# A recurrence's spilled tiles: later loads in longer pieces, values at the sixth phase, scales for two units at a time

## The chip, the cores and the metric

The kernel runs on one core of one Trainium2 chip. The metric is the device time of one execution in microseconds (us). TensorE (PE) multiplies matrices, VectorE (DVE), ScalarE (ACT) and GpSimd (POOL) work element by element, and SyncE (SP) issues nearly all DMAs. "PEld" in the profile is TensorE's loading of the stationary operand, which overlaps its matmuls.

## The reference

The model has two layers over 256 tokens of width 2048: an RWKV-7 mixer with a recurrent state per head, and a sparse attention mixer. Only the first layer's recurrence and what feeds it matter here. It is, per head of size 64:

```
def wkv7_scan(r, w, k, v, a, b):
    def step(S, inp):
        r_t, w_t, k_t, v_t, a_t, b_t = inp
        sa = einsum('bhvk,bhk->bhv', S, a_t)
        S = S * w_t[:, :, None, :] + sa[..., None] * b_t[:, :, None, :] + v_t[..., None] * k_t[:, :, None, :]
        return S, einsum('bhvk,bhk->bhv', S, r_t)
    ...
o = (o - mean) * rsqrt(var + GN_EPS) * ln_g + ln_b
o = (o + sum(r * k * r_k) * v) * silu(z)
y = o @ w_o
```

There are 32 heads. The projections r, k, v, z are products of the mixed input with four 2048x2048 matrices, and `w_o` is another.

## The kernel before, in words

The kernel computes in chunks of 64 tokens, four chunks in all, so the recurrence turns into small matmuls. Two column blocks of 128 (four heads) make a **unit**; there are eight units, U = 0 to 7, and x = 0 or 1 names a block in a unit. An earlier stage has already made, for every block, a tile with four parts (transformed keys, cumulated decays, a scaled key and the removal vectors) and has **spilled** it to DRAM as `spd`, 128 rows of 1284 values each. The values v and the gate z lie in DRAM as `vd` and `zd`.

The recurrence's loop runs over units, and in each over 12 **phases** v = 0 to 11: three for each chunk. In a phase the program writes, one after the other, the phase's own small matmuls with their copies (`phase`), the preparation of the next unit (`prep`), the normalization of the unit before (`finish`), loads, and then `fill(n)`, which puts in n steps of dense matmuls: first the projection r (`pair_block`, lines L1249 to L1251), then the output product. In this part the instructions of all five engines stay in the order in which the program writes them. SP is an engine like the others here: a DMA whose turn has not come, because the one ahead of it waits, is not issued.

What the change touches and what reads it:

- `load_spl` (L998, L1002) brings the spilled tile of unit U into `SPL[U % 2]`. Unit 0 and unit 1 come before the loop, each as two whole tiles of 642 KB. In the loop unit U + 2 comes during unit U, one piece of a fifth of a tile in each of the phases 0 to 9. The first 512 of the 1284 columns are read by `prep` steps "B0" and "B1" (phases 2 and 4 of the unit before), the rest by `scale_r` (L1035 to L1038, phase 6 of the unit before) and by steps "A0" and "A1" behind it (L1080, L1082, phases 7 and 9).
- `load_v` (L1007) brings the values of unit U + 1 into `UV` in phase 0 of unit U; the matmuls L1097 read them from phase 0 of unit U + 1.
- `load_gb` brings `a_ln_g` and `a_ln_b`, repeated over 64 partitions, into `gb` (runs of 64 values, 256 bytes). In unit 0, phases 8 to 11, it loads those of units 0 to 5; those of units 6 and 7 come in phase 10 of units 2 to 5. Steps "b" (L1181) and "g" (L1183) of the unit after read them.
- `load_rows` (L1019, L1021) brings v and z again for the normalization, in phases 8 and 9. Its first DMA waits for the unit before to be done with the tile.
- The weights come as pieces `wraw` of 512 KB (L179) into five buffers; ACT makes the high part `whi` of each (L207) and DVE the low part `wlo` (L192), three half-pieces ahead of the matmuls. A new piece can be issued when DVE has read the old one in its buffer.

While the first units run, DVE also works off a triangular inversion in the background (L849 to L885).

Of the kernel before, what the change touches and what calls it, by code (L numbers as in the profile page):

```python
# [218 lines left out]
def hybrid_kernel(ctx: ExitStack, tc: tile.TileContext, a: dict, out: bass.AP):  # L219
    nc = tc.nc  # L220
# [48 lines left out]
    def store_heads(d, nb, tt, t, eng):  # L269
        for i in range(2):  # L270
            dst = bass.AP(tensor=d.tensor, offset=d.offset + 4 * nb * 128 * T + (2 * tt + i) * CH,
                          ap=[[T, 64], [64 * T, 8], [1, 64]])
            eng.dma_start(dst, t[64 * i:64 * i + 64, :].rearrange("p (n d) -> p n d", d=64))
# [52 lines left out]
    for ph in QZ:  # L326
        if ph < 10:
            c0 = 128 * QB0[ph]
# [212 lines left out]
    def prep(kp):  # L541
        if kp == 2:
            banks(tp=(6,))
        px = turned_x[kp] if kp < 2 else turn_x(kp)
        for i in range(2) if kp else ():
            k = 2 * kp + i
            sl = px[:, i * 256:i * 256 + 256]
            norm_x(k, sl, G)
# [150 lines left out]
    SPW = 512 + NCH * (CH + 1) + 256 + 256  # L699
# [206 lines left out]
    H = lambda x, h: R[h ^ x]  # L906
    NU = NK // 2
# [6 lines left out]
    def load_a(U, which="AT"):  # L914
        sch.require(lambda: "T" not in which or U // 4 in tdone)
        for x in range(2):
            for h in range(2):
                j, at = 2 * U + x, 64 * (h ^ x) + 32
                if "A" in which:
                    d = abdd[j // 8][1]  # L920
                    src = bass.AP(tensor=d.tensor, offset=d.offset + (j % 8 * 8 + h) * 2048, ap=[[32, 32], [4096, NCH], [1, 32]])
                    G.dma_start(A10[at:at + 32, x, :, 0:32], src)
                if "T" in which:
                    G.dma_start(T00[64 * h:64 * h + 32, x, :, 0:32], inverse(tnd[U // 4], (j % 8) * 2 + h, 0))

    def load_y(U, eng=G, qs=(1, 0)):
        sch.require(lambda: U // 4 in tdone)
        for q in qs:
            for x in range(2):
                for h in range(2):  # L930
                    at = 64 * (h ^ x) + 32 * q
                    eng.dma_start(Yb[U % 2][at:at + 32, x, :, 32 * q:32 * q + 32],
                                inverse(yvd[U // 4], ((2 * U + x) % 8) * 2 + h, q))
# [54 lines left out]
    each = [(x, h) for x in range(2) for h in range(2)]  # L988
# [1 line left out]
    in_order = ExitStack()  # L990
    in_order.enter_context(tc.manual_schedule(engines={e.engine for e in (PE, V, S, G, nc.sync)}))

    SPLIT = (0, 256, 512, 772, 1028, SPW)

    def load_spl(U, pieces=range(10)):
        if len(pieces) == 10:
            for x in range(2):
                nc.sync.dma_start(SPL[U % 2][x][:, :SPW], spd[2 * U + x])  # L998
            return
        for i in pieces:  # L1000
            x, c0, c1 = i // 5, SPLIT[i % 5], SPLIT[i % 5 + 1]
            nc.sync.dma_start(SPL[U % 2][x][:, c0:c1], spd[2 * U + x][:, c0:c1])  # L1002

    def load_v(U, eng=nc.sync):
        for x in range(2):
            for h in range(2):
                eng.dma_start(UV[U % 2][R[h], 1 - x, h], vd[2 * U + x, R[h], :].rearrange("p (c d) -> p c d", c=NCH))  # L1007

    gb = one("gb", [128, 2, 12, 64])

    def load_gb(U, nu, part):
        for x, h in part:
            for i, v in enumerate((a["a_ln_g"][0], a["a_ln_b"][0])):
                src = bass.AP(tensor=v.tensor, offset=v.offset + U * 256 + x * 128 + h * 64, ap=[[0, 64], [256, nu], [1, 64]])
                nc.sync.dma_start(gb[H(x, h), i, x:2 * nu:2], src)

    def load_rows(t, d, U):
        flat = t.rearrange("p x c d -> p x (c d)")
        nc.sync.dma_start(flat[:, 0], d[2 * U])  # L1019
        for h in range(2):  # L1020
            nc.sync.dma_start(flat[H(1, h), 1], d[2 * U + 1, R[h]])  # L1021
# [8 lines left out]
    def scale_r(U, x):  # L1030
        if x == 0:
            PCH[U] = scan.tile([128, 2, NCH], F32, name="pc", bufs=3)
        BK, pp, kr, ar = parts(U, x)
        pr = rps[U % 2][:, 256 * x:256 * x + 256]
        V.tensor_tensor(ar[:, 1], c3(pr), pp[:, :, 1:], op=OP.mult)  # L1035
        V.tensor_tensor(mb[:, x], pr, kr, op=OP.mult)
        G.tensor_copy(PCH[U][:, x], pp[:, :, CH])
        G.tensor_tensor(ARS[U % 2][x], ar[:, :, 1:, :],  # L1038
                        pp[:, None, 0:NCH - 1, CH:CH + 1].to_broadcast([128, 2, NCH - 1, CH]), op=OP.mult)
# [103 lines left out]
    def stats(U, c):  # L1143
        if c == 0:
            STA[U] = (scan.tile([128, 2, 4, 6], F32, name="sta", bufs=2), scan.tile([128, 2, 4, 2], F32, name="mv", bufs=2))
        src = view(U, 192 + 64 * c, 64) if U == NU - 1 else OU[U][:, :, 64 * c:64 * c + 64]
        for x in range(2):
            V.bn_stats(STA[U][0][:, x, c, :], src[:, x])
# [44 lines left out]
    def turn_y(U):  # L1193
        yt = [PBK[U][:, x * 512:x * 512 + 256] for x in range(2)]
        for i in range(NCH):
            for x, h in each:
                r = H(x, h)
                PE.matmul(yt[x][R[h], i * 64:i * 64 + 64], OU[U][r, x, 64 * i:64 * i + 64], ident[r, r], start=True, **mm)
        made = [ring("y", 2 * U + x) for x in range(2)]
        for x, (yh, yl) in enumerate(made):  # L1200
            S.activation(yh, yt[x], AF.Copy)
            mixed[("y", 2 * U + x)] = (yh, yl)
        for x, (yh, yl) in enumerate(made):
            V.tensor_tensor(yl, yt[x], yh.bitcast(F32), op=OP.subtract)
        sch.t += 350
# [59 lines left out]
    def fill(n):  # L1265
        budget[0] += 3 * N256 * n
        while budget[0] > 1.0:
            c = next(dense)
            budget[0] -= c
            sch.t += c  # L1270
            sch.pump()

    W.late = True
    load_spl(0)
    load_y(0, G, (1,))
    load_a(0, "A")
# [8 lines left out]
    G.memset(Yb[1], 0.0)  # L1285
    load_y(1)
    fill(8)
    load_spl(1)
    fill(8)
    PBK[1] = pair_tile(1)  # L1290
    for step in PROLOGUE:
# [15 lines left out]
    for U in range(NU):  # L1307
        PBK[U] = pair_tile(U % 2)
        P = U - 1
        PACE[0] = PACES[min(U + 1, 3)]  # L1310
        for v in range(12):
            HOLD[0] = U > 0 and v in (0, 1, 2, 11)
            phase(U, v // 3, v % 3)
            if v % 3 == 2 and U == NU - 1:
                stats(U, v // 3)
            sch.pump()
            if v == 10 and U + 2 < NU:
                load_y(U + 2, qs=(1,))
            if v == 11:
                finish(U, "copy")  # L1320
                if U == NU - 1:
                    finish(U, "rg")
            if v == 0:
                if U and U + 1 < NU:
                    load_y(U + 1, qs=(0,))
                if U + 1 < NU:
                    load_v(U + 1)
            if U == 0 and v == 2:
                PACE[0] = 0.0
                for _ in range(9):  # L1330
                    sch.pump()
                PACE[0] = PACES[1]
            if v < 10 and U + 2 < NU:
                load_spl(U + 2, (v,))
            if v == 6 and U + 1 < NU:
                scale_r(U + 1, 0)
                scale_r(U + 1, 1)
            for step in AUX.get(v, ()):
                if step == "T":
                    if U:  # L1340
                        turn_y(P)
                elif U + 1 < NU:
                    prep(step, U + 1)
            if U:
                for step in NORM.get(v, ()):
                    finish(P, step)
            if v == 3 and U == 0:
                for tt in range(2):
                    store_heads(zd, 3, tt, z3[tt], G)
            if v > 7 and U == 0:  # L1350
                load_gb(0, 6, each[v - 8:v - 7])
            if v == 10 and U in (2, 3, 4, 5):
                load_gb(6, 2, each[U - 2:U - 1])
            if v == 5 and U + 2 < NU:
                load_a(U + 2, "AT" if U != 2 else "A")
            if v == 8 and U == 2:
                load_a(U + 2, "T")
            if v == 8:
                load_rows(vt, vd, U)
            if v == 9:  # L1360
                load_rows(zt, zd, U)
            fill(FILLO if U + 1 == NU else FILLL[v] if U + 2 == NU else FILL[v])
            sch.pump()
    U = NU - 1
# [541 lines left out]
```

## Time and profile before

| what | value |
|---|---|
| median of 3 runs | 1115.77 us (1111.92 to 1116.19) |
| profiled execution | 1113.02 us, its span 1111.2 us |
| granted TensorE clock | 0.998 |
| busy share of the span: PE, PEld, DVE, ACT, POOL | 98%, 86%, 76%, 65%, 31% |
| `spl` pieces in the loop | 60 DMAs of 128 or 130 KB |
| whole `spl` tiles ahead of the loop | 4 DMAs of 642 KB |

The recurrence lies between about 340 and 560 us of the span. A view "by windows" gives the busy time of each engine in each stretch; "waits" says what ended an engine's idle time; the "timeline" lists instructions by start, with the idle time ahead of them in brackets. "Landing" of a DMA is the time from its issue to its data being there. A matmul's modelled end lies some 0.16 us after the next one's start, so that short holes between matmuls do not show as idle time.

### The profile page before, as it was taken

How to read it: one execution, taken by the hardware profiler on the slowest of the kernel's cores; microseconds unless marked ns; L12 is line 12 of the kernel's file. 1: busy time of each engine (PE TensorE's matmuls, PEld its weight loads, DVE VectorE, ACT ScalarE, POOL GpSimd, SP SyncE). 2: the span in 40 equal slices, each digit the busy share in tenths (PEclk: the TensorE clock that was granted, in tenths of full speed). 3: DMA queues.
4: the chain of work that ended last, by engine and by line, in shares of the span. 5: the costliest groups of instructions: out<-in, count | busy, mean ns of one | idle time of the engine just before them, and what ended most of it. 6: DMA issues, size and time to landing. Idle time of an engine off the chain costs nothing.

```text
span 1111.2 us, 25246 instructions
## 1 busy us (share of the span) xinstructions
PE 1088.1 (98%) x9232; PEld 954.0 (86%) x9232; DVE 840.4 (76%) x1784; ACT 724.7 (65%) x1737; POOL 344.3 (31%) x423
## 2 busy tenths in 40 slices
PE   8999999999999899999999999999999999999997
PEld 7788899888889888999888888888989999988886
DVE  6999976679887897666667876765677988886564
ACT  7767777666775457656557766665657677775453
POOL 1300036424348557763200110101323334342012
PEclk9999999999999999999999999999999999999999
DMA  7458888877879968765578667675745354745753
GB/s 260 153 193 246 237 213 252 243 191 218 254 228 266 255 181 242 230 180 150 169 240 276 199 201 258 196 262 164 202 142 150 103 150 127 187 109 197 276 184 107
DMA packets 221837, 224.74 MB, mean 202 GB/s; under 512 B 48240, under 2 KB 173264, under 8 KB 221328
## 3 DMA queue, kind: packets, MB, share of 16 engines
q1 hardware_dynamic: 216384, 217.60, 65.9%
q0 software_dynamic: 4864, 4.92, 1.7%
q8 instruction: 73, 1.20, 0.5%
q10 hardware_dynamic: 464, 0.59, 0.2%
q14 instruction: 52, 0.43, 0.1%
HBM read 200.49 MB, written 22.58 MB: 201 GB/s over the span
## 4 chain that ended last, share of the span: by engine, by line
PE 57%; DVE 3%; ACT 1%; issue 1%; DMA 0%; POOLq 0%; POOL 0%; DVEq 0%; ACTq 0%
PE bank L617 8%; PE bank L616 8%; PE bank L619 8%; PE bank L1647 5%; PE bank L235 5%; PE bank L1648 3%; DVE wlo L192 2%; PE bank L1249 2%; PE bank L1250 1%; PE bank L1251 1%; PE pair L619 1%; PE pair L616 1%; PE pair L617 1%; PE bank L1215 1%; ACT whi L207 1%
## 5 line engine op out<-in xcount | busy, mean ns | idle before, releaser
L192 DVE TENSOR_TENSOR wlo<-wraw,whi 128x512 fp32r<-128x512 f32 (+2 forms) x616 | 443.8, 734 | 145.4 <-ACT whi L207 141.4
L207 ACT ACTIVATE whi<-wraw 128x512 fp32r<-128x512 f32 (+2 forms) x664 | 401.7, 618 | 180.8 <-PE bank L619 66.4
L192 POOL TENSOR_TENSOR wlo<-wraw,whi 128x512 fp32r<-128x512 f32 (+2 forms) x48 | 61.9, 1290 | 172.6 <-ACT whi L207 131.3
L617 PE MATMUL bank<-wlo,mh 128*128 128x512 f32 (+1 forms) x288 | 109.5, 382 | 1.3 <-DVE wlo L192 1.2
L617 PE MATMUL bank<-wlo,mhl 128*128 128x512 f32 (+2 forms) x288 | 108.0, 375 | 0.0
L619 PE MATMUL bank<-whi,ml 128*128 128x512 f32 (+1 forms) x288 | 107.9, 379 | 0.0
L619 PE MATMUL bank<-whi,mhl 128*128 128x512 f32 (+2 forms) x288 | 107.3, 373 | 0.0
L616 PE MATMUL bank<-whi,mhl 128*128 128x512 f32 (+2 forms) x288 | 99.5, 373 | 0.3 <-ACT Vt L1529 0.3
L616 PE MATMUL bank<-whi,mh 128*128 128x512 f32 (+1 forms) x288 | 91.9, 380 | 0.3 <-ACT whi L207 0.2
L1647 PE MATMUL bank<-mhl,whi 128*128 128x512 f32 x256 | 91.9, 397 | 0.0
L1249 PE MATMUL bank<-mhl,whi 128*128 128x256 f32 x256 | 77.9, 304 | 1.4 <-issue 1.4
L617 PE MATMUL bank<-wlo,kvh 128*128 128x512 f32 x192 | 76.0, 396 | 0.0
L619 PE MATMUL bank<-whi,kvl 128*128 128x512 f32 x192 | 75.3, 392 | 0.0
L634 PE MATMUL bank<-mh,whi 128*128 128x256 f32 x256 | 74.8, 292 | 0.4 <-ACT whi L207 0.4
L636 PE MATMUL bank<-mh,wlo 128*128 128x256 f32 x256 | 73.1, 288 | 0.6 <-DVE wlo L192 0.6
L635 PE MATMUL bank<-ml,whi 128*128 128x256 f32 x256 | 72.9, 285 | 0.0
L1648 PE MATMUL bank<-mhl,wlo 128*128 128x256 f32 x256 | 72.9, 285 | 0.0
L1251 PE MATMUL bank<-mhl,wlo 128*128 128x256 f32 x256 | 72.2, 282 | 0.2 <-DVE wlo L192 0.2
L1250 PE MATMUL bank<-mhl,whi 128*128 128x256 f32 x256 | 72.1, 282 | 0.0
L616 PE MATMUL bank<-whi,kvh 128*128 128x512 f32 x192 | 66.7, 391 | 0.0
L617 PEld LDWEIGHTS bank<-wlo,mh 128*128 128x128 f32 x288 | 54.1, 188 | 12.1 <-DVE wlo L192 2.5
L619 PEld LDWEIGHTS bank<-whi,ml 128*128 128x128 f32 x288 | 54.2, 188 | 9.5
(383 smaller groups left out, 2743.9 us busy)
## 6 DMA issues: line engine op xcount, KB each, us to landing
wraw<-in_a_w_rkvz_dram SPq DMA_DIRECT2D x128, 512.0 KB, 5.2
wraw<-in_kv_w_dram SPq DMA_DIRECT2D x48, 512.0 KB, 4.5
wraw<-in_b_w_in_dram SPq DMA_DIRECT2D x40, 512.0 KB, 4.3
wraw<-in_a_w_o_dram SPq DMA_DIRECT2D x32, 512.0 KB, 4.7
wraw<-in_b_w_o_dram SPq DMA_DIRECT2D x32, 512.0 KB, 4.2
spd<-sp SPq DMA_DIRECT2D x16, 642.0 KB, 4.9
wraw<-in_b_w_in_dram SPq DMA_DIRECT2D x24, 384.0 KB, 3.2
wraw<-in_cmp_w_dram SPq DMA_DIRECT2D x16, 512.0 KB, 3.9
```

Source lines behind the costliest of these rows:

```text
L192: eng.tensor_tensor(lv, src, hv.bitcast(F32), op=OP.subtract)
L207: self.nc.scalar.activation(hv, src, AF.Copy)
L616: PE.matmul(o, mh[:, ts], wh[:, 0, :], start=k == ends[0], stop=False)
L617: PE.matmul(o, mh[:, ts], wl[:, 0, :], start=False, stop=False)
L619: PE.matmul(o, ml[:, ts], wh[:, 0, :], start=False, stop=k == ends[1])
L634: PE.matmul(o, wh[:, s, :], mh, start=k == 0 and first, stop=False, **kw)
L636: PE.matmul(o, wl[:, s, :], mh, start=False, stop=k == NK - 1, **kw)
L1249: PE.matmul(oo, wh[:, i, c], mh, start=k == 0 and x == 0, stop=False, **kw)
L1250: PE.matmul(oo, wh[:, i, c], ml, start=False, stop=False, **kw)
L1251: PE.matmul(oo, wl[:, i, c], mh, start=False, stop=k == NK - 1, **kw)
L1647: PE.matmul(o, wh[:, s, :], beside[("u", k)], start=k == 0, stop=False)
L1648: PE.matmul(o[:, :T], wl[:, s, :], mh, start=False, stop=k == NK - 1)
```

## The change

The split of a tile is coarser: three pieces of 512, 516 and 256 columns in place of five. The pieces 0 and 3 (the first 512 columns of both blocks) of unit U + 2 are loaded in phases 6 and 8 of unit U. The other four are loaded in phases 0 to 3 of unit U + 1, the unit whose `scale_r` in phase 6 reads them. Unit 1 gets its pieces 0 and 3 ahead of the loop and the other four in unit 0, where it was loaded whole ahead of the loop. The values are loaded in phase 5 rather than 0. Units 0, 1 and 2 load `gb` for two units each in phases 8 to 11, where unit 0 loaded six.

```
-    SPLIT = (0, 256, 512, 772, 1028, SPW)
+    SPLIT = (0, 512, 1028, SPW)
...
-            x, c0, c1 = i // 5, SPLIT[i % 5], SPLIT[i % 5 + 1]
+            x, c0, c1 = i // 3, SPLIT[i % 3], SPLIT[i % 3 + 1]
...
-                nc.sync.dma_start(gb[H(x, h), i, x:2 * nu:2], src)
+                u0 = U % 6
+                nc.sync.dma_start(gb[H(x, h), i, 2 * u0 + x:2 * (u0 + nu):2], src)
...
-    load_spl(1)
+    load_spl(1, (0, 3))
...
-                if U + 1 < NU:
-                    load_v(U + 1)
...
-            if v < 10 and U + 2 < NU:
-                load_spl(U + 2, (v,))
+            if v < 4 and U + 1 < NU:
+                load_spl(U + 1, ((1, 2, 4, 5)[v],))
+            if v in (6, 8) and U + 2 < NU:
+                load_spl(U + 2, (3 * (v - 6) // 2,))
...
-            if v > 7 and U == 0:
-                load_gb(0, 6, each[v - 8:v - 7])
+            if v > 7 and U < 3:
+                load_gb(2 * U, 2, each[v - 8:v - 7])
...
+            if v == 5 and U + 1 < NU:
+                load_v(U + 1)
```

The order of instructions on PE, DVE, ACT and POOL is the same before and after; only SP's changes. SP, from the last loads ahead of the loop through unit 0 (`spl_4694` and `spl_4695` are the two blocks of odd units, `spl_4557` and `spl_4558` those of even ones), before:

```order
L998 DMA spl_4694<-spd 128x1284
L998 DMA spl_4695<-spd 128x1284
L179 DMA wraw<-in_a_w_rkvz_dram 128x4x256 x3
L1007 DMA uv_4698<-vd 64x256 x4
L1002 DMA spl_4557<-spd 128x256 x2
L179 DMA wraw<-in_a_w_rkvz_dram 128x4x256
L1002 DMA spl_4557<-spd 128x260
L1002 DMA spl_4557<-spd 128x256 x2
L1002 DMA spl_4558<-spd 128x256
L179 DMA wraw<-in_a_w_rkvz_dram 128x4x256
```

and now:

```order
L1002 DMA spl_4694<-spd 128x512
L1002 DMA spl_4695<-spd 128x512
L179 DMA wraw<-in_a_w_rkvz_dram 128x4x256 x3
L1002 DMA spl_4694<-spd 128x516
L1002 DMA spl_4694<-spd 128x256
L179 DMA wraw<-in_a_w_rkvz_dram 128x4x256
L1002 DMA spl_4695<-spd 128x516
L1002 DMA spl_4695<-spd 128x256
L1007 DMA uv_4698<-vd 64x256 x4
L179 DMA wraw<-in_a_w_rkvz_dram 128x4x256
```

Of unit 1's two tiles, two fifths stay ahead of the loop, and the rest takes the place where unit 2's pieces stood; the values follow behind them. SP in unit 4, from its last weight piece of the unit before to the weight piece of phase 5, before:

```order
L179 DMA wraw<-in_a_w_rkvz_dram 128x4x256
L1007 DMA uv_4698<-vd 64x256 x4
L1002 DMA spl_4557<-spd 128x256 x2
L179 DMA wraw<-in_a_w_rkvz_dram 128x4x256
L1002 DMA spl_4557<-spd 128x260
L1002 DMA spl_4557<-spd 128x256 x2
L1002 DMA spl_4558<-spd 128x256
L179 DMA wraw<-in_a_w_rkvz_dram 128x4x256
```

and now:

```order
L179 DMA wraw<-in_a_w_rkvz_dram 128x4x256
L1002 DMA spl_4694<-spd 128x516
L1002 DMA spl_4694<-spd 128x256
L179 DMA wraw<-in_a_w_rkvz_dram 128x4x256
L1002 DMA spl_4695<-spd 128x516
L1002 DMA spl_4695<-spd 128x256
L1007 DMA uv_4698<-vd 64x256 x4
L179 DMA wraw<-in_a_w_rkvz_dram 128x4x256
```

The pieces between the weight pieces are now those of unit 5, which the same unit's phase 6 reads, and no longer those of unit 6; the four loads of values have moved from ahead of them to behind them.

More of the change, by code (lines that the diff above doesn't have):

```diff
@@ L991, in hybrid_kernel, with load_spl @@
     in_order.enter_context(tc.manual_schedule(engines={e.engine for e in (PE, V, S, G, nc.sync)}))
-    SPLIT = (0, 256, 512, 772, 1028, SPW)
-    def load_spl(U, pieces=range(10)):
-        if len(pieces) == 10:
+    SPLIT = (0, 512, 1028, SPW)
+    def load_spl(U, pieces=None):
+        if pieces is None:
             for x in range(2):
```

## The prediction

> **What bounds the kernel now.** I read the page's first lines, then the busy time by windows over the recurrence, then TensorE's waits in it.
>
> ```profile
> span 1111.2 us, 25246 instructions
> PE 1088.1 (98%) x9232; PEld 954.0 (86%) x9232; DVE 840.4 (76%) x1784; ACT 724.7 (65%) x1737; POOL 344.3 (31%) x423
> ```
>
> TensorE is idle for 23.1 of 1111.2 us. The change moves DMAs of the recurrence alone, so what it can win lies there. Columns after the length: busy us of PE, PEld, DVE, ACT, POOL, then clock, DMA share, GB/s.
>
> ```profile
> 340.00:360.00 20.00, 20.00 (x273) 19.32 (x273) 13.63 (x29) 11.57 (x24) 16.00 (x32) 1.00 1.05 272
> 360.00:380.00 20.00, 18.52 (x397) 16.80 (x390) 16.64 (x57) 8.63 (x24) 10.48 (x19) 1.00 1.04 294
> 380.00:400.00 20.00, 18.61 (x377) 16.79 (x377) 16.89 (x49) 11.11 (x32) 12.94 (x18) 1.00 0.87 211
> 400.00:420.00 20.00, 17.84 (x390) 15.91 (x388) 19.50 (x46) 9.30 (x27) 9.83 (x16) 1.00 0.53 156
> 420.00:440.00 20.00, 19.98 (x425) 18.16 (x426) 16.92 (x40) 14.55 (x39) 13.85 (x25) 1.00 0.85 249
> 500.00:520.00 20.00, 20.00 (x381) 18.19 (x380) 12.66 (x35) 13.37 (x37) 10.51 (x15) 1.00 0.56 155
> ```
>
> From 420 us on TensorE has no idle time that shows: units 3 to 7 cannot be made faster by earlier data. From 360 to 420 us it is idle for 1.48 + 1.39 + 2.16 = 5.0 us. TensorE's waits between 340 and 560 us (total, times, longest) name them:
>
> ```profile
> PE bank L1082 <- issue: 1.4, 1, 1.4
> PE bank L1249 <- issue: 1.4, 1, 1.4
> PE pair L1198 <- DVE O L1187: 0.8, 1, 0.8
> PE pair L1097 <- DVE S L1134: 0.8, 1, 0.8
> PE pair L1120 <- ACT X L1115: 0.4, 1, 0.4
> PE bank L1251 <- DVE wlo L192: 0.2, 1, 0.2
> ```
>
> None of these is a wait for an `spl`, `uv` or `gb` load. Holes hidden under the overlapped matmul ends could add to the 5.0, so I check with the distance from one unit to the next. These rows start the first `scale_r` product of units 1 to 5:
>
> ```profile
> 375.19 0.41 DVE L1035 TENSOR_TENSOR spl<-bank,spl 128x256 f32<-128x256 f32 x1
> 399.48 0.41 DVE L1035 TENSOR_TENSOR spl<-bank,spl 128x256 f32<-128x256 f32 x1
> 424.90 0.41 DVE L1035 TENSOR_TENSOR spl<-bank,spl 128x256 f32<-128x256 f32 x1
> 446.72 0.43 DVE L1035 TENSOR_TENSOR spl<-bank,spl 128x256 f32<-128x256 f32 x1 [1.01 <-PE bank L1251]
> 469.35 0.42 DVE L1035 TENSOR_TENSOR spl<-bank,spl 128x256 f32<-128x256 f32 x1 [1.02 <-PE bank L1251]
> ```
>
> The distances are 24.3, 25.4, 21.8 and 22.6 us. The first two stand 2 × 22.2 = 44.4 against 49.7: an excess of 5.3 us by this measure, 5.0 by the other. About 5 us, 0.45%, is all that could be won.
>
> **What the change removes, and the gain.** The two holes put down to "issue" are 2.8 of the 5.0 us. Both fall where the DMA engines have no time left. The first three rows are those of the DMA view from 379 to 382 us, the last two TensorE's holes:
>
> ```profile
> DMA packets 1130, 0.54 MB, mean 181 GB/s; under 512 B 787, under 2 KB 1129, under 8 KB 1129
> q1 hardware_dynamic: 1099, 0.51, 110.1%
> q8 instruction: 1, 0.02, 3.4%
> 363.83 0.27 PE L1249 MATMUL bank<-mhl,whi 128*128 128x256 f32 x1 [1.37 <-issue]
> 383.15 0.21 PE L1082 MATMUL bank<-spl 64*64 64x64 f32 x1 [1.40 <-issue]
> ```
>
> One packet of instructions was on its way just ahead of the second hole, in a queue of its own, on engines that the data queue filled. I read the hole as TensorE out of instructions, which no row says outright.
>
> The change lightens this stretch. Ahead of the loop two loads of 642 KB become two of 256 KB (128 rows × 512 × 4 bytes): 0.77 MB less. In unit 0, four pieces of unit 1 and two of unit 2 make 0.77 + 0.51 MB, as much as unit 2's ten did. Eight `gb` loads of 96 KB become eight of 32 KB: 0.51 MB less, in 256-byte packets, which are most of the 787 above. The first part unloads the stretch before the first hole, the second the one at the second hole, where the DMA view counts 181 GB/s at full engines. Bounds: nothing, if the holes aren't the fetch, to 2.8 us, if both go. I take half, **1.4 us**, since the fetch still meets weight pieces and value loads there. The holes behind a DVE result (0.8 + 0.8 + 0.2) stay: in 400 to 420 us DVE is busy 19.50 of 20 us with the inversion, whose order isn't touched.
>
> [...]
>
> **What it adds.** Units 1 and 2 issue eight `gb` loads each that were not there, and the loop's pieces fall from 60 to 40, four of them unit 1's. In unit 1 SP stands idle where the new ones go:
>
> ```profile
> 410.39 1.09 SPq L1021 DMA_DIRECT2D zt<-zd  x2
> 414.94 0.39 SPq L179 DMA_DIRECT2D wraw<-in_a_w_rkvz_dram  x1
> L1015 SPq DMA_DIRECT2D gb<-in_a_ln_g_dram x8: 624/634/651, 376.2 to 502.5; - x8
> ```
>
> Six of the eight come after the wait for v's tile: 6 × 0.63 = 3.8 us against 414.94 − 411.48 = 3.5 idle. The weight piece is 0.3 us later, three half-pieces ahead of its use: no cost; with that cover gone it would be 0.3 us per unit, 0.6.
>
> **What it moves closer.** `scale_r` for block x = 1 needs piece 4, now issued in phase 2 behind the second weight piece of the unit. Unit 4 shows the distance; the last two rows are of DVE and TensorE, the others of SP:
>
> ```profile
> 459.96 2.60 SPq L1007 DMA_DIRECT2D uv<-vd  x4
> 463.84 0.38 SPq L179 DMA_DIRECT2D wraw<-in_a_w_rkvz_dram  x1
> 464.32 1.89 SPq L1002 DMA_DIRECT2D spl<-spd  x4
> 468.40 0.38 SPq L179 DMA_DIRECT2D wraw<-in_a_w_rkvz_dram  x1
> 473.39 0.29 DVE L1134 TENSOR_TENSOR S<-sP,pair 128x128 f32<-128x128 f32 x1 [2.02 <-PE pair L1129]
> 481.12 0.32 PE L1097 MATMUL pair<-uv,ama 64*64 64x64 f32 x8
> ```
>
> Piece 4 goes out at 464.3 at the latest (2.6 us earlier at best, with the value loads moved behind it). The second product of `scale_r` starts 0.67 us after the first, at 470.02: 5.7 us for the landing. If it is late, DVE stands, and queued behind it are a `wlo` and the state update S, which TensorE's next phase waits for; DVE is idle for 2.02 us ahead of S. So a landing up to 7.7 us costs nothing in units 3 to 6. Landings in the trace (the tile's range min/median/max; whole tiles; pieces):
>
> ```profile
> DMA to landing us min/median/max: 2.2/4.7/10.5
> spl<-spd SPq DMA_DIRECT2D x4, 642.0 KB, 7.3
> spl<-spd SPq DMA_DIRECT2D x48, 128.0 KB, 4.7
> ```
>
> A 258 KB piece lies between 4.7 and 7.3; I estimate 5.2, nearer to the small one. In units 0 to 2 DVE has no idle time, and the four-piece row of SP, the latest issue, stands at:
>
> ```profile
> 371.16 1.96 SPq L1002 DMA_DIRECT2D spl<-spd  x4
> 395.02 1.88 SPq L1002 DMA_DIRECT2D spl<-spd  x4
> 420.46 1.88 SPq L1002 DMA_DIRECT2D spl<-spd  x4
> ```
>
> The second products start at 375.86, 400.15 and 425.57, which leaves 4.7, 5.1 and 5.1 us. At 5.2 us it is late by 0.5 + 0.1 + 0.1 = 0.7; at 7.3 by 2.6 + 2.2 + 2.2 = 7.0; at 10.5 by 5.8 + 5.4 + 5.4 = 16.6; issued 2.6 us earlier, at 5.2, not at all. I take **0.4 us**. The x = 0 pieces are a weight piece ahead and cost nothing.
>
> The values go out behind piece 5, by 465.4 in unit 4, four issues in 2.6 us, and L1097 reads them at 481.12: 13 us for loads of 64 KB whose like landed in 4.7, so no cost; with a landing over 13 us TensorE would wait for the difference. The third weight piece, at 468.40, has the four value loads ahead of it: 464.3 + 1.0 + 2.6 = 467.9, still in time. The first 512 columns are loaded some 15 us before their transposes.
>
> **Sum.** Span: 1111.2 − 1.4 + 0.4 = 1110.2. The profiled execution took 1113.02, which is 2.75 under the median of the runs shown, so on that median the same step gives 1115.77 − 1.0 = **1114.8 us**.
>
> **Rivals.**
>
> - *The holes aren't the DMA engines' doing* (or others open in their place): 1115.8. For it: "issue" names no cause, and in 340 to 360 us TensorE had none with the DMA share at 1.05. Against it: in 420 to 560 us, with lighter DMA traffic, there is none.
> - *The whole early excess goes*, since DVE, 1.4 us earlier each time, no longer falls behind: 1115.8 − 5.0 = 1110.8. Against it: DVE's 19.50 of 20 us.
> - *Late pieces* (slower): piece 4 lands after DVE reaches `scale_r` in units 0 to 2, and everything behind it on DVE shifts with it. It decides above 4.7 to 5.1 us of landing, and above 7.7 us in the later units. Price 7.0 us at the 7.3 of whole tiles, 1122.8; 16.6 at the slowest seen, 1132. For it: at the median landing the margin is 0.0 to 0.4 us. Against it: the values no longer stand ahead, and the engines carry less there.
>
> **How the numbers follow.** Forecast 0.52, no gain 0.23, all of the excess 0.12, late pieces 0.13. Forecast and no gain are both within 0.5% of 1115.77 (1110.2 to 1121.3), which is about what a measurement of this kernel can tell from no change; the runs shown differ by 4.3 us among themselves. Faster takes half of the third case and a few hundredths of the first for that scatter: 0.10. Slower takes most of the last: 0.10. Within: 0.80. The range goes from 1109.5, the third case less some scatter, to 1121.5, short of the priced late pieces; the likeliest case alone has 1112 to 1118.
>
> **What would show it.** Right: no 1.4 us "issue" hole on TensorE between 360 and 385 us, or one; the distances of `scale_r` at 23 to 25, 25, then 22.6 us; DVE's L1035 never waiting for an `spl` DMA by more than about 0.5 us. Wrong: rows "DVE spl L1035 <- DMA spl" of a microsecond or more in several units, TensorE idle behind S (L1134) after 420 us, or `wlo` late behind weight pieces; on the other side, a drop over 5 us, which would mean that hidden holes in the later units were waits for data.

## The result, and the profile after

The changed kernel takes **1121.97 us** (median of 8 runs, 1117.6 to 1124.5) against 1115.84 of the kernel before on the same chip (8 runs, 1111.92 to 1116.78): ratio 1.0057, interval 1.0042 to 1.0072. It is slower by 6.1 us, and 0.5 us above the upper end of the range. The execution that was profiled took 1124.25 us, 11.2 more than the profiled one of before. So its trace shows about twice the median loss: it lies 2.3 us above its kernel's median, and the trace of before 2.8 below.

The page's first lines of the changed kernel:

```profile
span 1122.5 us, 25228 instructions
PE 1094.7 (98%) x9232; PEld 960.5 (86%) x9232; DVE 841.1 (75%) x1784; ACT 725.6 (65%) x1737; POOL 343.0 (31%) x423
```

TensorE is idle for 27.8 us instead of 23.1, and busy for 6.6 us more with the same 9232 matmuls: it also ran slower somewhere. The busy time by windows has both (columns as in the prediction: PE, PEld, DVE, ACT, POOL, clock, DMA share, GB/s):

```profile
360.00:380.00 20.00, 18.25 (x379) 16.57 (x378) 14.73 (x51) 8.90 (x25) 11.54 (x22) 0.91 0.84 242
380.00:400.00 20.00, 18.98 (x376) 17.23 (x372) 17.22 (x51) 9.80 (x28) 11.45 (x16) 1.00 0.71 205
440.00:460.00 20.00, 13.93 (x278) 12.44 (x277) 5.92 (x15) 9.93 (x28) 11.33 (x17) 0.86 0.72 181
460.00:480.00 20.00, 20.00 (x414) 18.22 (x415) 13.21 (x35) 11.13 (x31) 10.99 (x16) 0.97 0.66 180
```

The DMA engines got lighter in 360 to 400 us, as was reckoned (1.04 to 0.84, 0.87 to 0.71), and TensorE's idle time there stayed about what it was (2.8 of 40 us, 2.9 before). The new hole is in 440 to 460, where TensorE had 0.02 us of idle time before:

```profile
440.00:460.00 20.00, 19.98 (x466) 18.19 (x464) 12.70 (x29) 13.24 (x37) 15.22 (x24) 1.00 0.82 224
```

The waits between 340 and 560 us, after. Line numbers are one or two higher than before: `scale_r` is L1036 and L1037, the matmuls behind it L1081 and L1083, the dense ones L1250 to L1252.

```profile
PE bank L1083 <- DVE mb L1037: 6.1, 1, 6.1
PE bank L1250 <- issue: 1.8, 1, 1.8
PE bank L1083 <- issue: 1.0, 1, 1.0
DVE spl L1036 <- DMA spl<-spd: 8.0, 2, 6.6
```

The two "issue" holes are both still there, 1.8 + 1.0 in place of 1.4 + 1.4. One single wait is new, of 6.1 us: TensorE behind `scale_r`, and `scale_r` behind a piece of the spilled tile. Its place, by the rows that start `scale_r` in units 0 to 4 (in unit 3 also the one of block x = 1):

```profile
377.25 0.41 DVE L1036 TENSOR_TENSOR spl<-bank,spl 128x256 f32<-128x256 f32 x1
401.19 0.41 DVE L1036 TENSOR_TENSOR spl<-bank,spl 128x256 f32<-128x256 f32 x1
426.62 0.41 DVE L1036 TENSOR_TENSOR spl<-bank,spl 128x256 f32<-128x256 f32 x1
448.86 0.42 DVE L1036 TENSOR_TENSOR spl<-bank,spl 128x256 f32<-128x256 f32 x1 [1.41 <-DMA spl<-spd]
456.19 0.42 DVE L1036 TENSOR_TENSOR spl<-bank,spl 128x256 f32<-128x256 f32 x1 [6.58 <-DMA spl<-spd]
479.13 0.42 DVE L1036 TENSOR_TENSOR spl<-bank,spl 128x256 f32<-128x256 f32 x1 [1.02 <-PE bank L1252]
```

From unit 2 to unit 4 it is 479.13 − 426.62 = 52.5 us, against 469.35 − 424.90 = 44.45 before: 8.1 of the 11.3 us of span. The distance of the first two units, 23.9 us, is what it was (24.3), and so is that of the next (25.4). The rest of the 11.3 is small: 0.6 ahead of the loop, 1.5 in unit 0 (a stretch at half clock, shown at the end) less 0.3 in unit 1, and 1.4 behind unit 6.

**Why the piece was late** stands in SP's timeline. Before, around the end of unit 2:

```profile
435.20 0.63 SPq L1015 DMA_DIRECT2D gb<-in_a_ln_g_dram  x1
435.87 0.62 SPq L1015 DMA_DIRECT2D gb<-in_a_ln_b_dram  x1
...
437.90 0.39 SPq L179 DMA_DIRECT2D wraw<-in_a_w_rkvz_dram  x1
...
442.47 0.39 SPq L179 DMA_DIRECT2D wraw<-in_a_w_rkvz_dram  x1
443.19 2.52 SPq L1002 DMA_DIRECT2D spl<-spd  x4
```

and after (the last row is pieces 4 and 5, the row ahead of it the second weight piece):

```profile
438.24 1.65 SPq L1016 DMA_DIRECT2D gb<-in_a_ln_g_dram  x1
439.94 0.62 SPq L1016 DMA_DIRECT2D gb<-in_a_ln_b_dram  x1
...
442.56 0.60 SPq L1016 DMA_DIRECT2D gb<-in_a_ln_b_dram  x1
443.26 0.54 SPq L179 DMA_DIRECT2D wraw<-in_a_w_rkvz_dram  x1
443.85 1.78 SPq L1002 DMA_DIRECT2D spl<-spd  x2
...
446.20 0.38 SPq L179 DMA_DIRECT2D wraw<-in_a_w_rkvz_dram  x1
446.64 1.29 SPq L1002 DMA_DIRECT2D spl<-spd  x2
```

Unit 2 now issues ten `gb` loads: its own two of units 6 and 7 stay, and eight are added. Six of the ten stand in one row ahead of the weight piece, which goes out at 443.26 instead of 437.90, 5.4 us later where the unit itself is only 1.7 us later (by unit 2's `scale_r`). Everything behind it follows within 3.4 us: 512 KB, 258 + 128 KB, a bias of 24 KB, 512 KB, and then piece 4, issued at 446.64 and read by DVE from 456.19. The view "critical", which follows the work that ended last back to what released it, goes from TensorE's hole to this load and from it back through SP's issues, eight of `gb` among them. Its row of the load:

```profile
446.64 9.52 DMA spl<-spd
```

So the piece was late for two reasons: it was issued late, and its landing took 9.5 us. The second is not explained by the bytes ahead of it. In unit 4 of the same execution the same weight and spilled pieces go out in 3.6 us, from 468.60 on, and piece 4, issued at 472.16, lands in 5.5 us:

```profile
spl<-spd SPq DMA_DIRECT2D x1, 258.0 KB, 5.5
```

Windows of 2 us show that the DMA engines had little to do in the second half of the small loads (0.29 of their time in 440 to 442 as well). They were nearly full at 446 and from 450 to 458 (0.91 to 1.07), but not in between:

```profile
442.00:444.00 2.00, 2.00 (x57) 1.87 (x55) 1.14 (x2) 1.49 (x4) 2.00 (x2) 1.00 0.29 68
446.00:448.00 2.00, 2.00 (x29) 1.93 (x25) 0.89 (x2) 1.84 (x6) 2.00 (x5) 1.00 1.05 275
448.00:450.00 2.00, 2.00 (x37) 1.80 (x36) 0.76 (x2) 1.98 (x7) 2.00 (x4) 1.00 0.58 155
454.00:456.00 2.00, 0.00 (x0) 0.00 (x0) 0.00 (x0) 0.00 (x0) 0.00 (x0) 0.58 1.07 226
456.00:458.00 2.00, 1.00 (x28) 1.01 (x32) 1.35 (x3) 0.00 (x0) 0.35 (x2) 0.50 0.93 227
```

What stretched this landing stays open.

The same rows show the second part of the price: from about 454.3 us on the granted clock is one half (0.58 as the mean of 454 to 456), and until about 461.1 (0.97 as the mean of 460 to 480). Of this TensorE works from 457.0: its 61 matmuls from the start at 457.00 to the one at 461.17 took 4.16 us, and the same 61 before, from 449.05 to 451.39, 2.33, so this stretch cost 1.8 more. Together with the 6.1 of waiting that is about the 8.1. The lower clock is not that of one execution alone: its mean is 0.994 over the eight runs of the change, and 0.996 over the 89 runs of the kernel before in the experiments below. 0.002 of 1120 us would be some 2.2 of the 6.1 us, an estimate that takes TensorE to be at work in the slow stretches and to slow down as the clock does (2.1 us over the 4.1 us above, where its matmuls lost 1.8).

### The profile page after: what moved, and what is told of

Same layout as the page of the kernel before. It is cut to its first block, busy times and chain, and to the rows that moved or that the text cites. A ratio compares the mean times of both kernels' runs of the same rounds, so it can differ in the third digit from the quotient of the medians.

```text
span 1122.5 us, 25228 instructions
## 1 busy us (share of the span) xinstructions
PE 1094.7 (98%) x9232; PEld 960.5 (86%) x9232; DVE 841.1 (75%) x1784; ACT 725.6 (65%) x1737; POOL 343.0 (31%) x423
## 4 chain that ended last, share of the span: by engine, by line
PE 53%; DVE 4%; DMA 2%; ACT 2%; issue 1%; SPq 1%; POOLq 0%; POOL 0%; DVEq 0%; ACTq 0%
PE bank L617 8%; PE bank L619 8%; PE bank L616 8%; PE bank L1650 5%; PE bank L235 4%; PE bank L1651 3%; DVE wlo L192 2%; PE bank L1250 2%; PE pair L619 1%; PE pair L616 1%; PE pair L617 1%; PE bank L1251 1%; PE bank L1252 1%; ACT whi L207 1%; PE bank L1216 1%
## 5 line engine op out<-in xcount | busy, mean ns | idle before, releaser
L1250 PE MATMUL bank<-mhl,whi 128*128 128x256 f32 x256 | 78.9, 308 | 1.8 <-issue 1.8
L1252 PE MATMUL bank<-mhl,wlo 128*128 128x256 f32 x256 | 72.9, 285 | 0.2 <-DVE wlo L192 0.2
```

Source lines behind the costliest of these rows:

```text
L1250: PE.matmul(oo, wh[:, i, c], mh, start=k == 0 and x == 0, stop=False, **kw)
L1252: PE.matmul(oo, wl[:, i, c], mh, start=False, stop=k == NK - 1, **kw)
```

## The experiments

All kernels keep the order of instructions on TensorE, VectorE and ScalarE, and on GpSimd too but for one; what they change is what a queue issues, and when. Their ratios go by runs of the kernel before on the same chip in the same batch (medians 1115.91, 1116.15 and 1115.43 us; 22 to 34 runs). Two readings stood against each other at first: that the added `gb` loads delay the late pieces in SP's queue (theory A), and that the pieces are simply late wherever `gb` stands (theory B).

**1. Each part put back, or alone.** The change with `gb` loaded as before:

```
-            if v > 7 and U < 3:
-                load_gb(2 * U, 2, each[v - 8:v - 7])
+            if v > 7 and U == 0:
+                load_gb(0, 6, each[v - 8:v - 7])
```

> The changed kernel, but the normalization scales and biases loaded as before (six units at once in unit 0, eight loads in all in place of 24). Theory A (queue): the scales' loads that now stand in units 1 and 2 hold SP for about 5 us at the end of unit 2, and the weight piece and the four pieces of unit 4 behind them land after scale_r has been reached in unit 3; without them the loss goes: 1114 to 1117 us, and DVE's wait for an spl load is under 1 us in every unit. Theory B (distance): pieces that are loaded in the unit that reads them come too late by themselves, whatever stands ahead: 1120 to 1124 us, with a wait of some us at scale_r.

The kernel before with the new `gb` loads alone (and their new places in `gb`):

```
-            if v > 7 and U == 0:
-                load_gb(0, 6, each[v - 8:v - 7])
+            if v > 7 and U < 3:
+                load_gb(2 * U, 2, each[v - 8:v - 7])
```

> The kernel before with the scales and biases for two units at a time as the only edit. Theory A: SP falls behind by the same 5 us at the end of unit 2, but the pieces behind it are read a whole unit later, so it costs 0 to 1 us: 1115 to 1117. Theory B: the same. A third theory (C: the loads of scales cost by themselves, through later weight pieces) expects 1119 to 1123.

Measured: 1118.59 us, 1.0027 (1.0012 to 1.0042), and 1114.93 us, 0.9993 (0.9977 to 1.001). The added loads cost nothing by themselves, and without them half of the loss goes and with it the long wait (the longest left in `scale_r` for a piece is 0.5 us). The first time lies between the bands of the two theories, so neither has it alone. The loss of unit 3 needs both parts.

**2. Fewer loads in unit 2.** The last `gb` loads a unit later, so that unit 2 issues eight and not ten:

```
-            if v == 10 and U in (2, 3, 4, 5):
-                load_gb(6, 2, each[U - 2:U - 1])
+            if v == 10 and U in (3, 4, 5, 6):
+                load_gb(6, 2, each[U - 3:U - 2])
```

> The changed kernel with the loads of the last two units' scales in units 3 to 6 in place of 2 to 5, so that unit 2 issues eight of these loads and not ten. Theory A: the queue at the end of unit 2 is 1.2 us shorter (two issues of 0.6 us), so DVE's wait at scale_r in unit 3 goes from 6.6 us to 4 to 5.5 us: 1119.5 to 1121. Theory B: no change, 1121 to 1123.

1122.82 us, 1.0052 (1.0034 to 1.007): no better than the change, where theory A had expected 1119.5 to 1121. In its profiled execution, its fastest (1118.5 us), the longest wait for a piece is down to 3.7 us, but the median does not follow. In that execution the weight piece went out 1.4 us less late against unit 2's `scale_r`, and piece 4 2.9 us less late, at 441.21. The critical chain no longer passes through a `gb` load. But the landing was again a long one:

```profile
441.21 9.98 DMA spl<-spd
```

So with the `gb` loads off that chain a long landing still made DVE wait for 3.7 us. The times of this kernel, like those of the changed one, fall into two groups: of the changed kernel's eight, three stand at 1117.6 to 1119.5 and five at 1121.9 to 1124.5. I read this as the length of one wait varying from execution to execution. The landings of 5.5 to 10.0 us in the traces of this case would go with that, but only one execution of each kernel was traced, so it isn't shown.

**3. The pieces a unit earlier**, all else as in the change:

```
-    load_spl(1, (0, 3))
+    load_spl(1, range(6))
...
-            if v < 4 and U + 1 < NU:
-                load_spl(U + 1, ((1, 2, 4, 5)[v],))
+            if v < 4 and U + 2 < NU:
+                load_spl(U + 2, ((1, 2, 4, 5)[v],))
```

> The changed kernel with the four late pieces moved back by a whole unit (unit U loads all six pieces of unit U + 2, and unit 1 is loaded ahead of the loop); long pieces, values in phase 5 and scales two units at a time stay. Theories A and B both expect the loss to go, 1114 to 1117, with no wait for an spl load at scale_r. If it stays at 1120 or more, the pieces' lateness isn't the cause.

1116.64 us, 1.0009 (0.9994 to 1.0024). SP's queue is held up just as in the change, and the weight piece goes out as late, yet `scale_r` of unit 3 waits for no piece:

```profile
441.93 0.61 SPq L1016 DMA_DIRECT2D gb<-in_a_ln_b_dram  x1
442.64 0.54 SPq L179 DMA_DIRECT2D wraw<-in_a_w_rkvz_dram  x1
443.28 1.96 SPq L1002 DMA_DIRECT2D spl<-spd  x2
```

So a late weight piece costs little; the late pieces carry the loss.

**4. Earlier pieces and `gb` as before** (edits 1 and 3 together: only the longer pieces and the values' place are left), and **late pieces alone** (`gb` as before and the values in phase 0):

> The changed kernel with both undone: scales six units at once, and the four late pieces a unit earlier. What is left of the change is six longer pieces in place of ten and the values in phase 5. Theory A (the added scale loads hold SP, late pieces pay) and theory B (pieces too late by themselves) both expect the time before: 1114 to 1117 us. Under 1112 would mean that longer pieces win something that the rest of the change hid.

> The changed kernel with scales as before and the values back in phase 0: longer, later pieces are the only edit. It stands beside the run with scales as before (1118.6 us). Theory B now says that late pieces alone cost 2 to 3 us, in units 0 to 3, as they are behind the four loads of values again: 1118 to 1121, with a wait for an spl load at scale_r of 1 us or more in some unit. Theory A alone expects 1115 to 1117.

1117.66 us, 1.0018 (1.0006 to 1.003), and 1118.62 us, 1.0032 (1.0016 to 1.0049). The first is 0.7 us above the expected band. In the second, late pieces alone cost about half of what the change does, with waits for pieces of 2.4 us in all, 1.5 the longest: that is what theory B had expected.

**5. Who issues.** The `gb` loads from GpSimd's queue, where everything else is as in the change:

```
-                nc.sync.dma_start(gb[H(x, h), i, 2 * u0 + x:2 * (u0 + nu):2], src)
+                G.dma_start(gb[H(x, h), i, 2 * u0 + x:2 * (u0 + nu):2], src)
```

> The changed kernel with the 32 loads of scales and biases issued by GpSimd in place of SP: the same bytes in the same packets at the same places of the program, but SP is not held by them. Theory A in its form 'SP's issue time': SP has no 5 us of issues at the end of unit 2, the weight piece and the pieces go out then, and the wait at scale_r in unit 3 falls under 1.5 us: 1116 to 1119, like the run with scales as before. If it is the packets on the DMA engines that hold the pieces up, the wait stays at 3 us or more and the time at 1121 to 1124.

1123.29 us, 1.0073 (1.006 to 1.0087). SP's weight piece now goes out at 437.73 and the two pieces behind the second weight piece at 441.28, and `scale_r` waits for none: the same bytes and packets, issued elsewhere, make no piece late. But they now stand in front of GpSimd's own work. Its rows, and TensorE's:

```profile
442.94 0.62 POOL L1016 DMA_DIRECT2D gb<-in_a_ln_g_dram  x1 [3.48 <-issue]
...
445.86 0.59 POOL L1016 DMA_DIRECT2D gb<-in_a_ln_b_dram  x1
...
449.22 1.68 POOL L1172 TENSOR_TENSOR rg<-rg,half 128x8 f32<-128x8 f32 x1
452.20 0.49 PE L1098 MATMUL pair<-uv,ama 64*64 64x64 f32 x8 [3.76 <-DVE S L1135]
```

`rg` of the normalization starts at 449.22, and at 441.67 in the change. DVE waits 8.6 us for `rg`, and the state update S behind it on DVE holds TensorE for 3.8 us. So the wait followed the expectation for SP's issue time, and the time did not: the price has moved to another queue. The six loads ahead of `rg` take 3.5 us to issue, and the idle 3.5 us ahead of the first of them are put down to "issue"; how much of `rg`'s delay is issue time alone isn't shown.

**6. More of the same.** Eight more `gb` loads in unit 2 (those of units 2 and 3 a second time):

```
+            if v > 7 and U == 2:
+                load_gb(2, 2, each[v - 8:v - 7])
```

> The changed kernel with eight more loads of scales in unit 2 (those of units 2 and 3 a second time, into the same place): 18 in that unit in place of ten. Theory A: six of the eight lie behind the wait for v's tile, 6 x 0.63 = 3.8 us more of SP's time ahead of the weight piece and the pieces, so the wait at scale_r in unit 3 grows from 3 to 6.6 by 2 to 4 us, and with the clock's loss behind it the time is 1124 to 1129. Theory B: as the changed kernel, 1121 to 1123.

1124.67 us, 1.0086 (1.0069 to 1.0104). Both blocks' `scale_r` in unit 3 wait here, too (the first row is SP's issue of pieces 4 and 5):

```profile
449.86 0.98 SPq L1002 DMA_DIRECT2D spl<-spd  x2
...
452.20 0.42 DVE L1036 TENSOR_TENSOR spl<-bank,spl 128x256 f32<-128x256 f32 x1 [5.44 <-DMA spl<-spd]
455.38 0.42 DVE L1036 TENSOR_TENSOR spl<-bank,spl 128x256 f32<-128x256 f32 x1 [2.43 <-DMA spl<-spd]
```

7.9 us in all for 8 more loads, against 8.0 in the profiled execution of the change: the sum does not grow with the dose there, only the time does, by 2.7 us between medians. The weight piece was 3.4 us later (446.66), but piece 4, issued at 449.86 behind the same 1.4 MB in 3.2 us, landed in 5.5 us. The longer queue and the shorter landing offset each other, so a simple proportion to the loads is not borne out.

**7. The same loads elsewhere in the unit.** The `gb` loads in phases 4 to 7, ahead of SP's wait for v's tile, with the pieces late as in the change; and the same with the pieces a unit earlier:

```
-            if v > 7 and U < 3:
-                load_gb(2 * U, 2, each[v - 8:v - 7])
+            if 3 < v < 8 and U < 3:
+                load_gb(2 * U, 2, each[v - 4:v - 3])
```

> The changed kernel with the scale loads of units 0 to 2 issued in phases 4 to 7 of the same units instead of 8 to 11: the same loads, the same late pieces, but the eight loads stand ahead of SyncE's wait for v's tile, in time that it spends idle. Theory A (the loads hold SyncE's queue just ahead of the weight piece and the late pieces): the weight piece of the end of unit 2 goes out about 5 us earlier than in the changed kernel, no wait of scale_r for a piece over 1.5 us in unit 3, its step from unit 3 to unit 4 is 22.5 to 24.5 us instead of 30.3, and the time is 1117 to 1119.5, like the changed kernel with the scales loaded as before. Theory B (it is the number of the small loads and their 256-byte packets, wherever they are issued): the wait stays over 3 us and the time at 1121 to 1123.

> The changed kernel with the scale loads in phases 4 to 7 and all six longer pieces a unit earlier (unit 1's ahead of the loop), so that both of the parts that met are apart. Theory A: no wait for a piece, and 1115.5 to 1118, the level of the changed kernel with the pieces a unit earlier; it would beat the kernel before only if the longer pieces gave something, and no run so far shows that. Theory B: 1118 or more.

1118.46 us, 1.0029 (1.0013 to 1.0045), and 1115.24 us, 1.0001 (0.999 to 1.0012). The long wait is gone from the first:

```profile
443.67 0.39 SPq L179 DMA_DIRECT2D wraw<-in_a_w_rkvz_dram  x1
...
446.80 0.93 SPq L1002 DMA_DIRECT2D spl<-spd  x2
...
452.14 0.42 DVE L1036 TENSOR_TENSOR spl<-bank,spl 128x256 f32<-128x256 f32 x1 [1.02 <-PE bank L1252]
454.33 0.42 DVE L1036 TENSOR_TENSOR spl<-bank,spl 128x256 f32<-128x256 f32 x1 [1.43 <-DMA spl<-spd]
```

The first time is as theory A had expected (the second is 0.3 us under its band), and so is the step from unit 3 to unit 4, 23.4 us where the change has 30.3. That the weight piece would go out 5 us earlier was a miss on the span's own time, since this execution reached unit 3 some 3 us later (429.43 for unit 2's `scale_r`, 426.62 in the change). Against its own `scale_r` it went out 8.5 us ahead; before that was 8.8, and in the change 5.6, of which `scale_r` itself waited 1.4.

**8. What is left, taken apart.** The kernel before with the values in phase 5, and with three longer pieces in place of five in the units where they stood (the split is the change's, and unit 1 is loaded ahead of the loop in six pieces):

```
-                if U + 1 < NU:
-                    load_v(U + 1)
...
+            if v == 5 and U + 1 < NU:
+                load_v(U + 1)
```

> The kernel before with one part of the change alone: the values loaded in phase 5 rather than phase 0. With the longer pieces a unit early and the scales as before the time stood at 1.0018 of the kernel before, and nothing that I read accounts for it. If the values' place does it, this kernel is at 1117 to 1118.5; if it costs nothing, as the prediction said, it is at 1115 to 1116.5.

```
-            if v < 10 and U + 2 < NU:
-                load_spl(U + 2, (v,))
+            if v < 4 and U + 2 < NU:
+                load_spl(U + 2, ((1, 2, 4, 5)[v],))
+            if v in (6, 8) and U + 2 < NU:
+                load_spl(U + 2, (3 * (v - 6) // 2,))
```

> The kernel before with one part of the change alone: three longer pieces of a tile in place of five, four of them in phases 0 to 3 and two in phases 6 and 8 of the unit that loaded them before; the values in phase 0, the scales as before. If the longer pieces cause the 1.0018 that was left, this kernel is at 1117 to 1118.5 with a step or a hole of TensorE in units 0 to 2 or 5 to 6 that the kernel before does not have; if not, it is at 1115 to 1116.5, and the values would have to be the cause.

1114.48 us, 0.9998 (0.9986 to 1.0009), and 1116.43 us, 1.0015 (1.0005 to 1.0026). The values' place is free (the time is 0.5 us under the band expected for that). The longer pieces cost 0.15% with the large `gb` loads in unit 0, and nothing that shows with the small ones in phases 4 to 7 (1.0001 above). The time of 1116.43 lies in the band that was expected if they cost nothing, so the 0.15% rests on the ratio's interval alone.

The runs side by side, as ratios to the kernel before (values in phase 5, or 0 where marked):

| `gb` | pieces in the unit that reads them | pieces a unit earlier |
|---|---|---|
| two units at a time, phases 8 to 11 | 1.0057 (the change) | 1.0009 |
| two units at a time, phases 4 to 7 | 1.0029 | 1.0001 |
| six units at once in unit 0 | 1.0027, and 1.0032 (phase 0) | 1.0018, and 1.0015 (phase 0) |

Row by row, late pieces cost 0.48, 0.28 and 0.09 to 0.17%; in the third row the intervals overlap. The first row's excess of 0.2 to 0.4% goes with the collision in unit 3. No version is clearly faster than the kernel before.

## Why the prediction was wrong, point by point

- **What bounds the kernel: right.** No wait for `spl`, `uv` or `gb` data in the kernel before, about 5 us to win in units 0 and 1. The cover that made the later units wait-free was the subject of the change, and there it fell.
- **The gain of 1.4: wrong.** The traces go with the reading of the two "issue" holes, without a row that says it: in every traced execution that has them they end at the same two matmuls, and in the traces of before and after a packet of 16,384 bytes in the instructions' own queue ends 1.5 and 1.7, and 1.4 and 1.3 us ahead of the holes' ends. What did not hold is that fewer bytes on the DMA engines shorten them. The DMA share fell as reckoned, and the holes are 2.8 us as before. In the window of the first, 362 to 365 us, the data queue still fills the engines:

```profile
q1 hardware_dynamic: 831, 0.83, 100.6%
q8 instruction: 1, 0.02, 2.4%
```

  The first rival (no gain) had this right. Most of these packets came without a hole: the trace of before has 73 in that queue (1.20 MB) and two "issue" holes on TensorE. In these two places the traces show holes of 0.2 to 2.2 us.
- **What it adds: the step that failed.** It counted "eight `gb` loads each" in units 1 and 2, looked at SP in unit 1, and priced the weight piece alone, 0.3 us late. Unit 2 issues ten, six of them in a row, and the weight piece at its end went out 3.6 us later against the unit's own course (5.36 less 1.72); unit 2 was the one to look at. And the weight piece was the wrong thing to price: late weights cost little (the pieces a unit earlier, 1.0009), the spilled pieces behind them were what somebody waited for. The added loads by themselves are free, as reckoned (0.9993).
- **What it moves closer: the term of 0.4 us failed with it.** It put nothing on units 3 to 6, and unit 3 lost 8.1 us in the trace, 6.1 of them TensorE's wait. Three inputs were off. "A landing up to 7.7 us costs nothing in units 3 to 6" took the issue times of the kernel before: in unit 3 the issue was 446.64, 2.2 us ahead of `scale_r`'s first product and not 5.0. The landing took 9.5 us rather than 5.2; why isn't shown, since the same loads ahead came with 5.5 in unit 4. And the slack of 2.0 us ahead of the state update S is not there: TensorE waited for `mb` (L1037), the last product of `scale_r`, and of DVE's 6.6 us it waited 6.1. In the run with `gb` in phases 4 to 7, too, 0.5 of 1.4 us reach TensorE, so that the slack is 0.5 to 0.9 us. The first block's piece, priced at nothing, held DVE for 1.4 us. In units 0 to 2, where 0.4 us were taken and the rival put 7 us, nothing waited; in units 4 to 6 nothing did either. The two sections were each priced against the old SP queue, and neither against the queue that the other one makes.
- **The values: right**, no cost (0.9998).
- **The rival of late pieces** had the mechanism with the wrong place: it needed slow landings in units 0 to 2, and said of the later units only that it decides above 7.7 us of landing. That its price (1122.8) is near the result is luck.
- **The distances** for units 0 to 2 came as forecast. Of the signs named as wrong, DVE's wait for an "spl" DMA came, in one unit and not in several. TensorE's hole stood behind `mb` and not behind S.

**What stays open.** What makes the same piece land in 5.5 or in 10 us is not known; the wait in unit 3 needs both the late issue and the long landing to reach 6.6 us. Late pieces without the collision still cost 0.28% (1.0029 against 1.0001), some 3 us. The traces show a longest wait for a piece of 0.5 to 1.5 us, of which at most 0.6 reach TensorE, and in the profiled execution with `gb` in phases 4 to 7 a half-clock stretch of 6.8 us at the first hole where its partner has 3.4 us, which is an estimated 1.4 us, by what 3.4 us cost in the change. Over all their runs the mean granted clocks are 0.9948 (11) and 0.9968 (12), and 0.0020 of 1118 us is an estimated 2.2 us: most of the difference goes with the clock, but why late pieces should lower it is not settled. Why the longer pieces cost 0.15% beside the large `gb` loads is not settled either; three of the four traces with both have a second "issue" hole of 1.68 to 1.80 us with a half-clock stretch, and the fourth one of 1.24 without.

## What to carry to other kernels

When several loads move, write out the queue that results, in the unit where most of them meet, and price every load against that queue and not against the old one. What a small DMA cost the issuing queue here was its issue time, 0.6 us for 32 KB, and what stood behind it paid; issued from GpSimd's queue, GpSimd's own work came late in its place (`rg` at 449.22 for 441.67). A load just ahead of its use has to allow for the spread of its landing as well as for its issue: the same piece behind the same loads took 5.5 to 10.0 us in these traces.

## What the runs showed of the hardware

**A hole of 1.75 us came with a stretch at half clock.** After the first "issue" hole of the changed kernel, 1.75 us long, the clock is at a half for 3.4 us (the row of the matmul that ends the hole, and windows of 2 us):

```profile
364.81 0.28 PE L1250 MATMUL bank<-mhl,whi 128*128 128x256 f32 x1 [1.75 <-issue]
```

```profile
364.00:366.00 2.00, 1.19 (x9) 1.18 (x8) 1.76 (x10) 0.00 (x1) 1.06 (x2) 0.89 1.11 284
366.00:368.00 2.00, 2.00 (x16) 1.66 (x16) 1.90 (x7) 1.06 (x3) 1.70 (x3) 0.50 1.11 290
368.00:370.00 2.00, 2.00 (x25) 1.80 (x25) 0.98 (x5) 0.00 (x0) 0.00 (x0) 0.76 0.83 223
```

By these rows the clock was at a half for 0.4 + 2.0 + 1.0 = 3.4 us. The 21 matmuls from the start at 365.52 to the one at 368.98 took 3.46 us, and the same 21 before, from 364.54 to 366.56, 2.02, a loss of 1.4: nearly as much again as the hole. Over the traces of this case "issue" holes up to 1.57 us at this place and 1.40 at the second came with none (the kernel before: 1.37 and 1.40), holes of 1.75 us and more always came with one, and 1.58 to 1.69 went either way. Where windows or rows show its start, the slow stretch begins between 0.4 us ahead of the hole's end (with `gb` in phases 4 to 7) and some 1.5 us behind it. With `gb` as before there are two such in one execution, the first with 6.8 us:

```profile
366.65 0.37 PE L1250 MATMUL bank<-mhl,whi 128*128 128x256 f32 x1 [2.24 <-issue]
388.34 0.27 PE L1083 MATMUL bank<-spl 64*64 64x64 f32 x1 [1.68 <-issue]
```

So in these traces the recurrence's holes have a step in their price: the first one of the change, 1.75 us long and not 1.37, cost 1.8 us more, 0.4 of hole and 1.4 of slow stretch. What sets the step isn't shown, and a slow stretch is not tied to such holes alone: one of 3.4 us begins at 249.5 us of the changed kernel's execution, ahead of the recurrence and behind waits of 0.6 and 0.7 us, where the kernel before has waits of up to 0.7 us and the full clock. Which of two executions gets the longer hole is not set by the change alone: the kernel before with the new `gb` loads alone has the same program up to there, and a first hole of 1.96 us.

**The small loads cost issue time more than bandwidth.** One `gb` load of 32 KB held SP for 0.6 us in the median, a weight piece of 512 KB for 0.4 to 0.5. Over the last four of the six small ones in a row, 440 to 444 us, the DMA engines stood at 0.29 of their time.
